# Norm sums taken one token to a partition and turned back, and GpSimd's three scalings issued in a row

## The chip, the core and the metric

The kernel runs on one core of one Trainium2 chip. The metric is device time in microseconds (us), from the start of an execution to its end; smaller is better. One execution was also recorded by the hardware profiler, and all rows below come from it. The engines are named as the profile names them: PE is TensorE (matmuls), PEld its weight loads, DVE VectorE, ACT ScalarE, POOL GpSimd, SP the engine that issues the transfers.

## The reference, cut to what matters

A two-layer backbone over 256 latent tokens (`x`) and 256 context tokens (`xc`), width 1024. Each layer is FFN, token mixer, FFN; in front of each of the three stands an RMS norm with a learned shift and scale. Layer 0 mixes with latent attention (MLA), which norms two of its inner projections as well; layer 1 with windowed attention. In the last layer the context stream is dropped after the mixer.

```python
def rms_norm(x, g):
    xf = x.astype(jnp.float32)
    y = xf * lax.rsqrt(jnp.mean(xf * xf, axis=-1, keepdims=True) + EPS)
    return (y * g.astype(jnp.float32)).astype(x.dtype)

def modulate(h, shift, scale):
    return h * (1.0 + scale) + shift
...
    for layer in range(DEPTH):
        x = x + 0.5 * mx[2] * swiglu(modulate(rms_norm(x, norm_g[layer, 0]), mx[0], mx[1]), ...)
        xc = xc + 0.5 * mc[2] * swiglu(modulate(rms_norm(xc, norm_g[layer, 0]), mc[0], mc[1]), ...)
        hx = modulate(rms_norm(x, norm_g[layer, 1]), mx[3], mx[4])
        hc = modulate(rms_norm(xc, norm_g[layer, 1]), mc[3], mc[4])
        ox, oc = mla_mixer(hx, hc, ...) or swa_mixer(hx, hc, ...)
        x = x + mx[5] * ox
        x = x + 0.5 * mx[8] * swiglu(modulate(rms_norm(x, norm_g[layer, 2]), mx[6], mx[7]), ...)
        if not last:
            ...
    return rms_norm(x, final_norm_g)
```

In `mla_mixer` the projections `cq` (512 wide) and `ckv` (256 wide) go through `rms_norm` before they are multiplied on.

## The kernel before

Everything is held transposed: features on the 128 partitions, tokens along the free axis. `xs[d]` (d = 0 to 7) holds 128 features of all 512 tokens; columns 0 to 255 are the latent stream, called stream 0 here, columns 256 to 511 the context stream, stream 1. Every product is done as three matmuls of two-part numbers (`mm3`, lines 210 to 212: high by high, high by low, low by high), so each weight tile is split into `whi` (ACT, line 182) and `wlo` (DVE or POOL, line 183), and each activation likewise.

`closing` runs the last projection of a sublayer tile by tile, adds it to `xs[d]` (line 357), and lets ACT square the new `xs[d]` (line 236) while POOL adds the squares up (line 242). The last two tiles are held back and done stream by stream. As soon as stream 0 is complete, the norm of the next sublayer starts for it while PE still works on stream 1: `rstd_of` multiplies the squares by a matrix of ones (line 221), so that every partition gets the sum for every token, ACT takes the root over 128x256 (line 223), DVE the reciprocal over 128x256 (line 225). `stream` then scales the eight tiles k = 0 to 7. For k = 2, 5, 7 (`POOL`) this is a product on POOL (line 287), gain and shift on ACT (line 288), and the split on ACT (line 182) and POOL (line 183); for the others DVE does product and gain (line 290), ACT adds the shift into the high part (line 185), and DVE makes the low part (line 186). Then `leading` multiplies the first weight tiles of the next sublayer by these inputs, k by k.

The norm appears fourteen times in this form. Six places in the program hold ten of them: place 1 (about 402 to 430 us, in front of MLA), place 2 (619 to 645, in front of the second FFN), place 3 (998 to 1020, first FFN of layer 1), place 4 (1374 to 1400, in front of the windowed attention) with both streams each, place 5 (1533 to 1550, last FFN, stream 0 alone) and place 6 (from 1734, the final norm, stream 0 alone, whose scaled tiles are written out). The other four are the inner norms of MLA (`Normed.finish`, 442 to 470). The very first norm of the program is coded apart.

A scheduler orders the instructions of each engine when the program is built; on the chip each engine runs its own list in order and waits for semaphores of the others. Buffers come from rings: 8 PSUM banks, 7 `strip` tiles of 128x256, 46 `r2k` tiles.

Of the kernel before, what the change touches and what calls it, by code (L numbers as in the profile page):

```python
# [10 lines left out]
F32 = mybir.dt.float32  # L11
# [3 lines left out]
ALU = mybir.AluOpType  # L15
# [22 lines left out]
def hybrid_backbone_kernel(ctx, tc, t, out):  # L38
# [6 lines left out]
    def bank(shape=(P, 512)):  # L45
        return ps.tile(list(shape), F32, tag="bank", name="bank")

    def r2k(n=512, parts=P):
        return ring.tile([parts, n], F32R, tag="r2k", name="r2k", bufs=46)
# [4 lines left out]
    def strip():  # L54
        return ring.tile([P, T], F32, tag="strip", name="strip", bufs=7)
# [107 lines left out]
    def behind(ins):  # L163

        return tc.issue_after(ins.ins) if ins else nullcontext()
# [48 lines left out]
    def pair(p, *idx):  # L214
        return p[0][idx], p[1][idx]

    def rstd_of(parts, dim, after=None):

        b = bank()[:, :T]
        for i, p in enumerate(parts):  # L220
            nc.tensor.matmul(b, lhsT=ones, rhs=p, start=(i == 0), stop=(i == len(parts) - 1))
        r = strip()
        nc.scalar.activation(r, b, AF.Sqrt, scale=1.0 / dim, bias=eps)  # L223
        with behind(after):
            nc.vector.reciprocal(r, r)  # L225
        return r

    class Squares:

# [19 lines left out]
    class Sublayer:  # L249
# [12 lines left out]
                self.squares[s].add(xs[d][:, SL[s]])  # L262

        def rstd(self, s):
            return rstd_of(self.squares[s].parts, D, self.end)

        def place(self, s, k):
            if k == len(self.hs):
# [8 lines left out]
            return mod[self.l][:, s, c:c + 1]  # L277

        def stream(self, s):
            r = self.r.get(s) or self.rstd(s)  # L280
            ys = {}

            def scale(k):
                ys[k] = r2k(T).bitcast(F32)
                x = xs[k][:, SL[s]]
                if k in POOL:
                    nc.gpsimd.tensor_tensor(ys[k], x, r, ALU.mult)  # L287
                    nc.scalar.activation(ys[k], ys[k], AF.Identity, bias=self.shift(s, k), scale=self.gain(s, k))
                else:
                    nc.vector.scalar_tensor_tensor(ys[k], x, self.gain(s, k), r, ALU.mult, ALU.mult)  # L290

            scale(0)
            for k in range(KT):
                if k + 1 < KT:
                    scale(k + 1)
                hi, lo = self.place(s, k)
                if k in POOL:
                    split(hi, lo, ys[k], engine=nc.gpsimd)
                else:
                    self.end = split(hi, lo, ys[k], bias=self.shift(s, k))  # L300
            return r[:, 0:1]
# [38 lines left out]
    class Final(Sublayer):  # L340


        def stream(self, s):
            r = self.rstd(s)
            for k in range(KT):
                y = strip()
                if k in POOL:
                    nc.gpsimd.tensor_tensor(y, xs[k][:, SL[s]], r, ALU.mult)
                    nc.scalar.activation(y, y, AF.Copy, scale=fng[:, k:k + 1])
                else:  # L350
                    nc.vector.scalar_tensor_tensor(y, xs[k][:, SL[s]], fng[:, k:k + 1], r, ALU.mult, ALU.mult)
                nc.sync.dma_start(out[k], y)
# [186 lines left out]
    def mla(sl, nxt):  # L539
# [3 lines left out]
        class Normed:  # L543
# [12 lines left out]
                    self.squares[s].add(raw[:, SL[s]])  # L556

            def finish(self, s):
                r = rstd_of(self.squares[s].parts, self.n * P)
                for i, x in enumerate(self.tiles):  # L560
                    if s == 0:
                        self.pairs.append((r2k(), r2k()))
                    hi, lo = self.pairs[i]
                    y = strip()
                    nc.vector.scalar_tensor_tensor(y, x[:, SL[s]], self.g[:, i:i + 1], r, ALU.mult, ALU.mult)
                    split(hi[:, SL[s]], lo[:, SL[s]], y)
                return r[:, 0:1]

# [414 lines left out]
```

## Time and profile before

| | |
|---|---|
| median of 3 runs | 1747.94 us (1747.8 to 1748.0) |
| profiled execution, its own time | 1748.32 us |
| its span, first to last instruction | 1746.3 us |
| PE busy | 1688.0 us (97%) |
| DVE, ACT, POOL busy | 62%, 38%, 11% |

The span is 2.0 us shorter than the execution's time; that rest lies before the first and after the last instruction. A busy share is an average over the whole program. Apart from the first 65 us and the inside of the windowed attention (1405 to 1510 us), PE idles for more than a moment only at the places named above, so what the norms cost is read there, from PE's idle time and from what ended it.

### The profile page before, as it was taken

How to read it: one execution, taken by the hardware profiler on the slowest of the kernel's cores; microseconds unless marked ns; L12 is line 12 of the kernel's file. 1: busy time of each engine (PE TensorE's matmuls, PEld its weight loads, DVE VectorE, ACT ScalarE, POOL GpSimd, SP SyncE). 2: the span in 40 equal slices, each digit the busy share in tenths (PEclk: the TensorE clock that was granted, in tenths of full speed). 3: DMA queues.
4: the chain of work that ended last, by engine and by line, in shares of the span. 5: the costliest groups of instructions: out<-in, count | busy, mean ns of one | idle time of the engine just before them, and what ended most of it. 6: DMA issues, size and time to landing. Idle time of an engine off the chain costs nothing.

```text
span 1746.3 us, 23850 instructions
## 1 busy us (share of the span) xinstructions
PE 1688.0 (97%) x9428; PEld 1439.0 (82%) x9428; DVE 1088.4 (62%) x1592; ACT 669.7 (38%) x1121; POOL 187.6 (11%) x183
## 2 busy tenths in 40 slices
PE   7999999999999999999999999999999989989997
PEld 4688888888788898888888888888888888889997
DVE  4877576646767467856946474645433679755554
ACT  4422222234556353222222342222222577554443
POOL 1000000004132130000000220000000452110001
PEclk9999999999999999999999999999999999999999
DMA  9556355431212126644735245634322221145552
GB/s 339 173 199 192 129 192 180 157 121 55 85 49 73 49 84 201 206 145 156 219 126 170 93 143 183 216 114 158 103 97 86 89 84 51 55 145 181 173 191 96
DMA packets 72831, 242.71 MB, mean 139 GB/s; under 512 B 8848, under 2 KB 10640, under 8 KB 72720
## 3 DMA queue, kind: packets, MB, share of 16 engines
q1 hardware_dynamic: 72720, 241.20, 41.9%
q8 instruction: 74, 1.21, 0.3%
q14 instruction: 37, 0.30, 0.1%
HBM read 240.11 MB, written 1.05 MB: 138 GB/s over the span
## 4 chain that ended last, share of the span: by engine, by line
PE 55%; DVE 4%; ACT 2%; issue 1%; POOL 1%; DMA 0%; POOLq 0%; ACTq 0%; DVEq 0%
PE bank L210 18%; PE bank L211 18%; PE bank L212 18%; DVE small L444 1%; DVE r2k L183 1%; PE bank L157 1%; DVE wlo L183 0%; DVE strip L225 0%; POOL r2k L183 0%; ACT r2k L182 0%; POOL r2k L287 0%; DVE small L457 0%; PE bank L102 0%; ACT whi L182 0%; DVE x L464 0%
## 5 line engine op out<-in xcount | busy, mean ns | idle before, releaser
L210 PE MATMUL bank<-r2k,whi 128*128 128x512 f32 (+1 forms) x2610 | 918.4, 353 | 9.3 <-ACT r2k L185 4.7
L211 PE MATMUL bank<-r2k,whi 128*128 128x512 f32 (+1 forms) x2610 | 915.3, 351 | 9.8 <-POOL r2k L183 6.1
L212 PE MATMUL bank<-r2k,wlo 128*128 128x512 f32 (+1 forms) x2610 | 912.2, 350 | 4.1 <-POOL wlo L183 2.2
L182 ACT CAST whi<-wraw 128x1024 fp32r<-128x1024 f32 (+1 forms) x313 | 321.7, 1028 | 886.8 <-PE bank L211 527.8
L210 PEld LDWEIGHTS bank<-r2k,whi 128*128 128x128 f32 x2610 | 494.6, 190 | 89.9 <-ACT whi L182 9.2
L211 PEld LDWEIGHTS bank<-r2k,whi 128*128 128x128 f32 x2610 | 496.2, 190 | 78.8 <-POOL r2k L183 8.6
L212 PEld LDWEIGHTS bank<-r2k,wlo 128*128 128x128 f32 x2610 | 495.7, 190 | 69.4 <-POOL wlo L183 3.0
L183 DVE TENSOR_TENSOR wlo<-wraw,whi 128x1024 fp32r<-128x1024 f32 (+1 forms) x302 | 362.9, 1204 | 134.7 <-ACT whi L182 124.7
L151 DVE SCALAR_TENSOR_TENSOR big<-modraw,conds,big 128x1024 f32<-128x1024 f32 x196 | 242.2, 1279 | 13.9 <-DMA modraw<-in_modw 13.3
L357 DVE SCALAR_TENSOR_TENSOR x<-bank,mod,x 128x256 f32<-128x256 f32 x192 | 85.7, 478 | 179.9 <-PE bank L212 179.9
L242 POOL TENSOR_TENSOR strip<-strip 128x256 f32<-128x256 f32 x64 | 65.2, 1032 | 1137.1 <-ACT strip L236 1110.4
L418 DVE TENSOR_TENSOR tmp<-bank,tmp 128x512 f32<-128x512 f32 (+1 forms) x88 | 54.9, 624 | 179.6 <-PE bank L212 177.7
L183 DVE TENSOR_TENSOR r2k<-bank,r2k 128x512 fp32r<-128x512 f32 (+2 forms) x107 | 62.0, 616 | 18.2 <-ACT r2k L182 17.9
L182 ACT CAST r2k<-bank 128x512 fp32r<-128x512 f32 (+2 forms) x107 | 52.4, 541 | 16.4 <-PE bank L212 15.7
L183 DVE TENSOR_TENSOR r2k<-tmp,r2k 128x512 fp32r<-128x512 f32 (+1 forms) x88 | 54.4, 618 | 1.5 <-ACT r2k L182 1.4
L182 ACT CAST r2k<-tmp 128x512 fp32r<-128x512 f32 (+1 forms) x88 | 49.7, 566 | 9.9 <-DVE tmp L418 9.5
L416 ACT ACTIVATE tmp<-bank 128x512 f32<-128x512 f32 (+1 forms) x88 | 47.3, 538 | 6.8 <-PE bank L212 6.8
L444 DVE TENSOR_REDUCE small<-bank 128x1 f32<-128x512 f32 (+1 forms) x64 | 37.7, 614 | 0.3 <-PE bank L645 0.2
L236 ACT ACTIVATE strip<-x 128x256 f32<-128x256 f32 x80 | 30.5, 410 | 17.9 <-DVE x L357 17.0
L225 DVE RECIPROCAL strip<-strip 128x256 f32<-128x256 f32 x14 | 24.5, 1750 | 19.9 <-ACT strip L223 19.9
L186 DVE SCALAR_TENSOR_TENSOR r2k<-r2k,mod 128x256 fp32r<-128x256 f32 x45 | 30.3, 696 | 8.7 <-ACT r2k L185 8.5
L450 ACT ACTIVATE tmp<-bank,small 128x512 f32<-128x512 f32 x32 | 21.9, 688 | 18.4 <-DVE small L446 12.3
(152 smaller groups left out, 1067.1 us busy)
## 6 DMA issues: line engine op xcount, KB each, us to landing
wraw<-in_win SPq DMA_DIRECT2D x172, 512.0 KB, 3.5
modraw<-in_modw SPq DMA_DIRECT2D x128, 512.0 KB, 4.2
wraw<-in_wout SPq DMA_DIRECT2D x64, 448.0 KB, 3.3
wraw<-in_wout SPq DMA_DIRECT2D x32, 512.0 KB, 3.5
r2k<-in_modo SPq DMA_DIRECT2D x32, 256.0 KB, 5.7
wraw<-in_mwo SPq DMA_DIRECT2D x8, 512.0 KB, 3.5
wraw<-in_swq SPq DMA_DIRECT2D x8, 512.0 KB, 3.5
wraw<-in_swo SPq DMA_DIRECT2D x8, 512.0 KB, 3.4
```

The costliest lines, as they stand in the source:

```text
L151: nc.vector.scalar_tensor_tensor(acc[s], raw, conds[:, kt, s:s + 1], acc[s], ALU.mult, ALU.add)
L182: nc.scalar.copy(hi, src)
L183: return engine.tensor_tensor(lo, src, hi.bitcast(F32), ALU.subtract)
L210: nc.tensor.matmul(o, lhsT=ah, rhs=bh, start=(i == 0), stop=False)
L211: nc.tensor.matmul(o, lhsT=ah, rhs=bl, start=False, stop=False)
L212: nc.tensor.matmul(o, lhsT=al, rhs=bh, start=False, stop=(i == n - 1))
L236: nc.scalar.activation(q, x, AF.Square)
L242: nc.gpsimd.tensor_tensor(self.parts[0], self.parts[0], q, ALU.add)
L357: nc.vector.scalar_tensor_tensor(xs[d][:, SL[s]], o[:, SL[s]], mod[l][:, s, c:c + 1], xs[d][:, SL[s]], ALU.mult, ALU.add)
L416: nc.scalar.activation(sg[:, :w], og[:, :w], AF.Silu)
L418: nc.vector.tensor_tensor(pr[:, :w], ou[:, :w], sg[:, :w], ALU.mult)
L444: nc.vector.tensor_reduce(top[:, j:j + 1], o[:, :w], axis=AX.X, op=ALU.max)
```

## The change

`rstd_of` now uses the squares as the weights of the matmul and one column of ones as the moving operand. The sum for 128 tokens then stands in one column with one token to a partition; two halves of 128 tokens and two parts of squares make four matmuls. Root and reciprocal are taken over 128x2. Each of the two columns is then spread over 128 columns and turned by a PE transpose against the identity, which gives the old layout in the upper half of the same bank (`wide`). ACT copies it to a `strip` (`kept`). The first tile (k = 0) is scaled from the bank, the others from the strip. In `stream`, POOL's three products for k = 2, 5, 7 are written in a row, right behind tile 0. The fixed position of the reciprocal behind an earlier instruction (`behind(after)`) is gone.

```diff
-    def rstd_of(parts, dim, after=None):
-
-        b = bank()[:, :T]
-        for i, p in enumerate(parts):
-            nc.tensor.matmul(b, lhsT=ones, rhs=p, start=(i == 0), stop=(i == len(parts) - 1))
-        r = strip()
-        nc.scalar.activation(r, b, AF.Sqrt, scale=1.0 / dim, bias=eps)
-        with behind(after):
-            nc.vector.reciprocal(r, r)
-        return r
+    def rstd_of(parts, dim):
+
+
+        b = bank()
+        for j in range(2):
+            for i, p in enumerate(parts):
+                nc.tensor.matmul(b[:, j:j + 1], lhsT=p[:, j * P:(j + 1) * P], rhs=ones[:, 0:1], start=(i == 0), stop=(i == len(parts) - 1))
+        r = small(2)
+        nc.scalar.activation(r, b[:, 0:2], AF.Sqrt, scale=1.0 / dim, bias=eps)
+        nc.vector.reciprocal(r, r)
+        wide = b[:, T:]
+        for j in range(2):
+            nc.tensor.transpose(wide[:, j * P:(j + 1) * P], r[:, j:j + 1].to_broadcast([P, P]), ident)
+        kept = strip()
+        nc.scalar.copy(kept, wide)
+        return wide, kept
...
         def stream(self, s):
-            r = self.r.get(s) or self.rstd(s)
+            wide, r = self.r.get(s) or self.rstd(s)
             ys = {}
 
             def scale(k):
-                ys[k] = r2k(T).bitcast(F32)
-                x = xs[k][:, SL[s]]
                 if k in POOL:
-                    nc.gpsimd.tensor_tensor(ys[k], x, r, ALU.mult)
                     nc.scalar.activation(ys[k], ys[k], AF.Identity, bias=self.shift(s, k), scale=self.gain(s, k))
                 else:
-                    nc.vector.scalar_tensor_tensor(ys[k], x, self.gain(s, k), r, ALU.mult, ALU.mult)
+                    ys[k] = r2k(T).bitcast(F32)
+                    nc.vector.scalar_tensor_tensor(ys[k], xs[k][:, SL[s]], self.gain(s, k), r if k else wide, ALU.mult, ALU.mult)
 
             scale(0)
+            for k in POOL:
+                ys[k] = r2k(T).bitcast(F32)
+                nc.gpsimd.tensor_tensor(ys[k], xs[k][:, SL[s]], r, ALU.mult)
             for k in range(KT):
...
             def finish(self, s):
-                r = rstd_of(self.squares[s].parts, self.n * P)
+                wide, r = rstd_of(self.squares[s].parts, self.n * P)
...
-                    nc.vector.scalar_tensor_tensor(y, x[:, SL[s]], self.g[:, i:i + 1], r, ALU.mult, ALU.mult)
+                    nc.vector.scalar_tensor_tensor(y, x[:, SL[s]], self.g[:, i:i + 1], r if i else wide, ALU.mult, ALU.mult)
```

The lists of the engines differ only around the norms; that of SP, which issues the transfers, is the same row by row. Three stretches show what moves. Rows of the new kernel carry its own line numbers: 221 became 223 (sums) and 229 (transposes), 223 became 225 (root), 225 became 226 (reciprocal), 231 is the new copy, 236 became 242, 242 became 248, 287 became 299 (POOL's product), 288 became 291, 290 became 294.

POOL at place 2, stream 0, before; the first row adds a square of stream 1 (`strip`), L287 multiplies by the norm, L183 makes a low part (`r2k`):

```order
L242 TENSOR_TENSOR strip<-strip 128x256 [waits Activation_49]
L287 TENSOR_TENSOR r2k<-x,strip 128x256 [waits DVE_49,PE_49]
L183 TENSOR_TENSOR r2k<-r2k 128x256 [waits PE_49,Activation_49]
L287 TENSOR_TENSOR r2k<-x,strip 128x256 [waits PE_49]
L183 TENSOR_TENSOR r2k<-r2k 128x256 [waits PE_49,Activation_49]
L287 TENSOR_TENSOR r2k<-x,strip 128x256
L183 TENSOR_TENSOR r2k<-r2k 128x256 [waits PE_49,Activation_49]
```

POOL at the same place in the new kernel:

```order
L248 TENSOR_TENSOR strip<-strip 128x256 [waits Activation_49,Pool_49] x9
L299 TENSOR_TENSOR r2k<-x,strip 128x256 [waits DVE_49,Activation_49]
L299 TENSOR_TENSOR r2k<-x,strip 128x256 [waits DVE_49] x2
L183 TENSOR_TENSOR r2k<-r2k 128x256 [waits PE_49,Activation_49]
L248 TENSOR_TENSOR strip<-strip 128x256 [waits Activation_49,Pool_49]
L183 TENSOR_TENSOR r2k<-r2k 128x256 [waits PE_49,Activation_49] x2
```

The three products moved ahead of stream 1's square and of the low parts that stood between them.

ACT at place 2, stream 0, from the first shift (L185) on, before:

```order
L185 ACTIVATE r2k<-r2k,mod_90 128x256 [waits DVE_49] x2
L288 ACTIVATE r2k<-r2k,mod_90,coefA_92 128x256 [waits Pool_49]
L182 CAST r2k<-r2k 128x256 [waits Activation_49]
L182 CAST whi<-wraw 128x1024 [waits DMAHW6_49,PE_49]
L185 ACTIVATE r2k<-r2k,mod_90 128x256 [waits DVE_49]
L236 ACTIVATE strip<-x 128x256 [waits DVE_49]
L185 ACTIVATE r2k<-r2k,mod_90 128x256 [waits DVE_49]
L288 ACTIVATE r2k<-r2k,mod_90,coefA_92 128x256 [waits Pool_49]
L182 CAST r2k<-r2k 128x256 [waits Activation_49]
```

ACT at the same place in the new kernel, from the copy (L231) on:

```order
L231 COPY strip<-bank 128x256 [waits PE_49,Pool_49]
L291 ACTIVATE r2k<-r2k,mod_90,coefA_92 128x256 [waits Pool_49]
L185 ACTIVATE r2k<-r2k,mod_90 128x256 [waits DVE_49]
L291 ACTIVATE r2k<-r2k,mod_90,coefA_92 128x256 [waits Pool_49]
L185 ACTIVATE r2k<-r2k,mod_90 128x256 [waits DVE_49]
L291 ACTIVATE r2k<-r2k,mod_90,coefA_92 128x256 [waits Pool_49]
L182 CAST r2k<-r2k 128x256 [waits Activation_49]
L242 ACTIVATE strip<-x 128x256 [waits DVE_49]
```

The gain-and-shift steps for POOL's tiles, which wait for POOL, moved ahead of the shifts of tiles 0 and 1, and the cast of tile 2 behind all three of them.

DVE at place 5, from the reciprocal on, before:

```order
L225 RECIPROCAL strip<-strip 128x256 [waits Activation_49]
L290 SCALAR_TENSOR_TENSOR r2k<-x,coefA_93,strip 128x256 [waits DVE_49]
L290 SCALAR_TENSOR_TENSOR r2k<-x,coefA_93,strip 128x256
L186 SCALAR_TENSOR_TENSOR r2k<-r2k,mod_91 128x256 [waits Activation_49] x2
L290 SCALAR_TENSOR_TENSOR r2k<-x,coefA_93,strip 128x256 x2
```

DVE at the same place in the new kernel:

```order
L226 RECIPROCAL small<-small 128x2 [waits Activation_49]
L294 SCALAR_TENSOR_TENSOR r2k<-x,coefA_93,bank 128x256 [waits Activation_49]
L294 SCALAR_TENSOR_TENSOR r2k<-x,coefA_93,strip 128x256
L186 SCALAR_TENSOR_TENSOR r2k<-r2k,mod_91 128x256 [waits Activation_49] x2
L294 SCALAR_TENSOR_TENSOR r2k<-x,coefA_93,strip 128x256 x2
```

The scaling of tile 0, which reads the bank, waits for ACT, one ACT instruction later than the reciprocal in front of it does: that is the copy into the strip.

## Rows read from the trace of the kernel before

**Rows 1.** The page's part 1: busy time, share of the span, instructions.

```profile
PE 1688.0 (97%) x9428; PEld 1439.0 (82%) x9428; DVE 1088.4 (62%) x1592; ACT 669.7 (38%) x1121; POOL 187.6 (11%) x183
```

**Rows 2.** PE's waits, the longest of a norm: who for whom, us, times, longest.

```profile
PE bank L211 <- POOL r2k L183: 6.1, 10, 1.2
```

**Rows 3.** Stretches: us, busy time by engine, PEclk (granted clock), DMA share, GB/s.

```profile
400.00:425.00 25.00, 22.84 (x165) 20.94 (x164) 14.58 (x21) 12.20 (x24) 9.17 (x11) 1.00 0.22 74
425.00:440.00 15.00, 12.98 (x94) 11.25 (x93) 12.17 (x17) 9.58 (x20) 5.36 (x6) 1.00 0.10 36
440.00:478.00 38.00, 38.00 (x187) 30.81 (x186) 28.79 (x47) 20.28 (x40) 4.63 (x5) 1.00 0.26 84
623.00:633.00 10.00, 8.90 (x68) 8.09 (x66) 7.88 (x15) 7.66 (x15) 4.83 (x6) 1.00 0.00 0
627.00:635.70 8.70, 6.33 (x43) 5.29 (x42) 5.42 (x8) 4.72 (x10) 4.86 (x5) 1.00 0.17 55
635.80:639.20 3.40, 3.40 (x16) 3.22 (x15) 1.75 (x1) 0.47 (x1) 0.00 (x0) 0.50 0.45 159
1380.00:1392.00 12.00, 9.71 (x67) 8.17 (x66) 11.21 (x15) 6.96 (x14) 6.90 (x9) 1.00 0.27 89
1530.00:1550.00 20.00, 14.66 (x94) 13.04 (x94) 11.45 (x16) 11.54 (x20) 7.02 (x8) 0.83 0.24 80
```

**Rows 4.** Groups by line and shape: count, busy us, mean ns, idle before.

```profile
L225 DVE RECIPROCAL strip<-strip 128x256 f32<-128x256 f32 x14 | 24.5, 1750 | 19.9 <-ACT strip L223 19.9
...
L221 PEld LDWEIGHTS bank<-strip,ones 128*128 128x128 f32 x56 | 9.5, 193 | 3.6 <-ACT strip L236 2.1 <-POOL strip L242 0.2
...
L223 ACT ACTIVATE strip<-bank,eps 128x256 f32<-128x256 f32 x14 | 6.6, 472 | 15.0 <-PE bank L221 15.0
...
L459 DVE RECIPROCAL small<-small 128x2 f32<-128x2 f32 x32 | 5.2, 162 | 8.9 <-ACT tmp L450 8.5
...
L456 ACT ACTIVATE small<-small,c_sink 128x2 f32<-128x2 f32 x16 | 4.7, 294 | 0.0
...
L102 PEld LDWEIGHTS bank<-c_ident,tmp 64*128 64x128 f32 x16 | 1.3, 138 | 1.4 <-issue 1.4
...
L791 ACT COPY tmp<-bank 128x256 f32<-128x256 f32 x2 | 0.7, 374 | 0.0
```

**Rows 5.** Timeline, PE: a norm's two sums; two transposes. Start, us.

```profile
422.09 0.28 PE L212 MATMUL bank<-r2k,wlo 128*128 128x256 f32 x1
422.21 1.02 PE L221 MATMUL bank<-strip,ones 128*128 128x256 f32 x4
...
683.27 0.39 PE L212 MATMUL bank<-r2k,wlo 128*128 128x512 f32 x1
683.50 0.60 PE L102 MATMUL bank<-c_ident,tmp 128*128 128x128 f32 x4
```

**Rows 6.** Timeline, weight loads of two small float32 transposes (64 columns moving).

```profile
1062.40 0.33 PEld L102 LDWEIGHTS bank<-c_ident,tmp 64*128 64x128 f32 x4 [0.35 <-issue]
```

**Rows 7.** Timeline, POOL at place 2, stream 0.

```profile
625.23 0.92 POOL L287 TENSOR_TENSOR r2k<-x,strip 128x256 f32<-128x256 f32 x1
...
631.00 0.92 POOL L287 TENSOR_TENSOR r2k<-x,strip 128x256 f32<-128x256 f32 x1
633.07 1.65 POOL L183 TENSOR_TENSOR r2k<-r2k 128x256 fp32r<-128x256 f32 x1 [1.15 <-DVE wlo L183]
```

**Rows 8.** Timeline at places 2 and 5: root, reciprocal, and the first work behind.

```profile
621.12 0.47 ACT L223 ACTIVATE strip<-bank,eps 128x256 f32<-128x256 f32 x1 [0.85 <-PE bank L221]
...
1536.20 0.46 ACT L223 ACTIVATE strip<-bank,eps 128x256 f32<-128x256 f32 x1
1536.69 1.75 DVE L225 RECIPROCAL strip<-strip 128x256 f32<-128x256 f32 x1 [0.97 <-ACT strip L223]
1539.56 0.80 PE L210 MATMUL bank<-r2k,whi 128*128 128x256 f32 x2 [4.03 <-ACT r2k L185]
...
1547.85 0.39 PE L211 MATMUL bank<-r2k,whi 128*128 128x256 f32 x1 [0.42 <-POOL r2k L183]
```

More of the change, by code (lines that the diff above doesn't have):

```diff
@@ L264, in rstd @@
         def rstd(self, s):
-            return rstd_of(self.squares[s].parts, D, self.end)
+            return rstd_of(self.squares[s].parts, D)
         def place(self, s, k):
@@ L343, in stream @@
         def stream(self, s):
-            r = self.rstd(s)
+            _, r = self.rstd(s)
             for k in range(KT):
```

## The prediction

> **What bounds the kernel now.** I read the page's busy times first. PE works 1688.0 us of the 1746.3 us span [rows 1], so 58 us are all that a shorter chain can win unless PE's own work shrinks. The waits of PE come next: the largest that belongs to norms is for POOL's low parts (line 183), 6.1 us in ten pieces [rows 2]; the longest single one is 4.03 us for the first shifted tile at place 5 [rows 8]. Then the stretches, to see where that idle time lies [rows 3]. PE idles 25.00 − 22.84 = 2.16 us at place 1 under stream 0's norm and 2.02 us under stream 1's; 2.37 us at place 2, which place 3 repeats nearly to the row; 2.29 us at place 4; 5.34 us at place 5. Around MLA's four inner norms (440 to 478) it idles 0.00 us. At place 6 nothing is left for PE; the chain itself ends the program. So ten norms can give something back and four can only cost.
>
> The same stretches show the granted clock. From 635.8 to 639.2 us it was 0.50, that is 1.2 instead of 2.4 GHz, with PE busy all the time, behind a stretch with 2.37 us of idle [rows 3]. Work that takes 3.4 us at half clock takes 1.7 at full, so this drop costs 1.7 us. Place 3 has one more like it, at the same point. At place 5 the mean clock is 0.83 over 20 us, which is 20 × 0.17 × 2 = 6.8 us at half clock, partly idle.
>
> **The reciprocal's chain.** Old: root 0.47, reciprocal 1.75, hand-over 0.04 [rows 4, 8], together 2.3 us from the sums to a usable norm. New: root over 128x2, for which the nearest row is another two-column ACT step, 0.29; reciprocal over 128x2, 0.16, the same shape in the softmax; two transposes, 0.60 from first start to last end [rows 4, 5]; the copy of a 128x256 bank, 0.37 [rows 4]; four hand-overs, some 0.05 each. Sum 1.6 us, 0.7 less. Tile 0's direct read of the bank gives nothing on top: in the new order DVE waits for the copy before that read, as the rows of DVE in the section on the change show. Had it not, tile 0 would come 0.4 us earlier.
>
> **PE's own work.** A norm's two old sums cost PE 0.86 us: four records that end at 422.21 + 1.02 = 423.23, where the matmul ahead ended at 422.37 [rows 5]. Two transposes cost 683.50 + 0.60 − 683.66 = 0.44 us by the same reading [rows 5]. The four new sums stream one column each, so their eight records (float32 takes two) are bound by loading 128 weight columns. The trace has no such matmul. From below: in the four small transposes at 1062.40 the weight loads start (0.33 − 0.14)/3 = 0.063 us apart [rows 6], 0.14 being one load [rows 4]. From above: a weight load of the old sums takes 0.193 us if nothing overlaps [rows 4]. I take 0.063, the same float32 load of 128 columns with little streaming behind it: 8 × 0.063 + 0.44 − 0.86 = +0.08 us a norm, with 0.193 +1.12 us. Fourteen norms: +1.2 us, at most +15.7.
>
> The Trainium skill (TensorE: Matmul & The Clock Gate, section "LDWEIGHTS (loading the stationary operand)") puts a load at columns / 1.2, so about 107 ns for 128 columns; the loads of [rows 6] start closer together than that. By that rule a norm would cost PE 0.86 + 0.44 − 0.86 = 0.44 us more, 6.2 us over fourteen.
>
> Where the transposes stand matters too, because PE runs its list in order and would stop at them for DVE. At places 1 to 4 stream 0's stand five products (0.6 us) behind the sums, and root plus reciprocal with hand-overs need about 0.6: at most 0.1 or 0.2 us of waiting each, which I count in the gains below. In MLA ten or seven long products (2.3 or 1.6 us) lie between, and DVE has at most one weight's low part ahead of the reciprocal. I count no wait there.
>
> **POOL and ACT at place 2, the pattern of places 1 to 4 (stream 0).** The root can start at 621.1 as before [rows 8]: the scheduler puts nine products instead of six between the two groups of sums, which the cheaper sums pay for. The norm is usable at 621.1 + 1.6 = 622.7. POOL's three products now follow at once, 0.92 each [rows 7]: 623.6, 624.5, 625.5, where the first started at 625.23 and the last at 631.00 before [rows 7]. But ACT's list now has a step for POOL's first tile ahead of the shift of tile 0, so nothing but the copy runs before 623.6; from there its fifteen instructions of this stretch take 7.7 us [rows 3] and the last cast ends at 631.3. POOL's last low part ends at 632.2 to 633.0 (0.92 like its other operations, or 1.65 beside DVE's weight splits as now [rows 7]); before it ended at 633.07 + 1.65 = 634.72, and PE waited for it. The input is 1.7 to 2.5 us earlier, PE has 2.37 us of idle to give; with some 0.5 us of waits left in between I count 1.8 us. Places 3 and 4 have like idle and the same lists around POOL: 1.8 each; place 1 has a little less: 1.6. Sum 7.0.
>
> Stream 1 at place 1 (2.02 us) gains little: there DVE now does four scalings in a row, beside POOL's three, before the first low part, so what the norm wins is spent in DVE's list. I count 0.2. At places 2, 3, 4 stream 1 is covered by the products of the third and fourth weight tiles or the next ones, and gains nothing.
>
> **Place 5.** The root starts at 1536.20, held by the load of ACT's table, not by the sums [rows 8]. The norm is usable at 1537.8 instead of 1538.44. Yet tile 0's shift now stands behind POOL's first product (0.92) and the ACT step on it (ACT's mean step is 7.66/15 = 0.5 [rows 3]), so PE starts near 1540.0, 0.4 later than 1539.56 [rows 8]. From there all inputs come faster than PE uses them. Its 48 products on them take 0.12 each at full clock, as the starts at 422.09 and 422.21 show [rows 5], 5.8 us in all. If the clock stays at half until about 1543.7 as it does now, 1.85 us of that is done by then and the rest ends at 1547.6. Today the last of these inputs comes at 1547.85 [rows 8] and four products follow, 1548.3. Gain 0.7 to 0.9, I take 0.9 since the last waits of ACT's casts go too. **Place 6** moves as a whole with the norm: 0.7.
>
> **Sum.** Gains 7.0 + 0.2 + 0.9 + 0.7 = 8.8. Costs: the seven norms without idle behind them (four in MLA, stream 1 at places 2 to 4) 7 × 0.08 = 0.6. Net 8.2 us. The execution profiled took 1748.32 (its span of 1746.3 and 2.0 around it), so 1740.1; the median shown, 1747.94, lies 0.4 below, so 1739.7 against it. The two drops to half clock (1.7 each) stand behind idle that shrinks from 2.4 to about 0.5; but place 1 had 2.0 us of idle in 15 and kept its clock [rows 3], so this is not certain either way. I count one of the two gone: **1738.0 us**. DVE loses 14 × 1.6 = 22 us of work, ACT 14 × 0.18 = 2.5 us of roots against 5.2 of copies; neither is the bound. No transfer is added or moved.
>
> **Rivals.**
> *A load of 128 full weight columns sets a pace of its own.* The two large transposes advance by 0.44/4 = 0.11 us a record [rows 5]. If that is their loads' pace and not that of their columns, the extra over 0.063 is 8 × 0.047 × 14 = 5.3 us: 1739.7 + 5.3 = 1745.0, no change that can be told. For it speaks that the trace has no one-column matmul, against it the spacing of [rows 6], where half the columns move. Chance 0.10. The rule of the Trainium skill named above comes to nearly this case.
> *ACT's list eats the gain.* If POOL's products run slow beside DVE (its low part beside DVE took 1.65 us [rows 7]), shifts of tiles 0 and 1 come a microsecond late and PE waits at the start instead of at the end: places 1 to 5 give nothing, place 6 0.7, costs 0.6: 1747.9. Against it: tile 0 and 1 have slack, since PE still works off stream 1. Chance 0.10.
> *Slower.* PE pays in full for the loads, 0.193 each, on its path at every norm: +15.7 − 8.8 = +6.9, 1754.8. It decides from the point where 14 × (8c − 0.42) exceeds 8.8 + 3.5 us, that is c = 0.16 us a load. Loads overlap in every row I read, so 0.06.
> *Forecast as above:* 0.74, with its own range 1733 (both drops and nearly all idle gone) to 1743 (neither drop gone, gains at half at two of the places).
>
> A measurement here can tell about 0.2%, 3.5 us, from no change, so from 1744.4 on it counts as the same. Faster: the forecast's 0.74 and a good third of the first rival's case, which straddles that line: 0.78. Same 0.16, slower 0.06. The range reaches up to the first rival and a little over: 1732 to 1746.
>
> **What would show it.** POOL's products at each place in one row of three, the third over by 626 at place 2; PE's idle there down from 2.37 to under 1 us; PE's time for the four sums near 0.5 us, the weight loads 0.06 apart; DVE's reciprocal at 0.16; PE's first product at place 5 no earlier than 1539.5 counted on the old time axis. Wrong it would be if the sums showed 0.1 us or more a load, if PE waited for DVE at the transposes for more than 0.2 us at a place, or if a new wait of PE for ACT's shifts of tiles 0 and 1 grew to what the wait for POOL was. A clock at half speed in a stretch that is at full speed now would also do it, at half of the stretch's length.

## The result, and the profile after

The changed kernel takes 1735.51 us (median; 1734.44 to 1736.61), the kernel before 1747.97 (1747.8 to 1748.78). The ratio is 0.9933 with a 95% interval of 0.992 to 0.9945: 12.5 us or 0.7% faster, where 1738.0 was predicted. The profiled execution took 1734.44, its span 1732.5.

The page's part 1, the answer to [rows 1]:

```profile
PE 1682.6 (97%) x9512; PEld 1440.9 (83%) x9512; DVE 1065.3 (61%) x1592; ACT 666.9 (38%) x1135; POOL 185.2 (11%) x183
```

The span fell by 13.8 us, PE's busy time by 5.4; the other 8.4 us are idle time that went. PE's waits (who for whom, us, times, longest), against [rows 2]:

```profile
PE bank L210 <- ACT r2k L185: 2.4, 1, 2.4
...
PE bank L229 <- DVE small L226: 2.1, 2, 1.0
...
PE bank L223 <- ACT strip L242: 1.9, 2, 1.0
...
PE bank L211 <- DVE r2k L186: 1.2, 1, 1.2
...
PE bank L211 <- POOL r2k L183: 0.7, 2, 0.4
```

The wait for POOL's low parts fell from 6.1 us in ten to 0.7 in two. New are waits for the reciprocal at the transposes (L229), 1.0 us each at places 5 and 6, where no product stands between.

The stretches that answer to [rows 3], moved to the new time axis by the offset of each place's first sum (columns as there): place 1, MLA, place 2 under stream 0, and what follows it, then place 5.

```profile
398.70:423.70 25.00, 24.41 (x187) 22.84 (x185) 14.40 (x26) 13.91 (x31) 11.29 (x15) 1.00 0.22 74
...
435.70:473.70 38.00, 38.00 (x207) 31.51 (x205) 22.38 (x47) 19.92 (x43) 4.58 (x5) 1.00 0.26 84
623.40:632.10 8.70, 8.27 (x67) 7.81 (x67) 5.62 (x10) 4.15 (x9) 3.28 (x5) 1.00 0.22 64
632.20:635.60 3.40, 3.40 (x31) 3.40 (x30) 3.40 (x5) 3.20 (x8) 2.76 (x4) 1.00 0.37 141
...
1518.00:1538.00 20.00, 15.61 (x110) 14.99 (x109) 10.36 (x16) 11.86 (x22) 6.91 (x8) 0.83 0.25 81
```

PE's idle time at place 2 went from 2.37 to 0.43 us, and the 3.4 us behind it run at a granted clock of 1.00 where [rows 3] has 0.50; PE runs 31 matmuls there instead of 16. Place 3 has lost its half-clock stretch too.

Groups by line and shape (count, busy us, mean ns, idle before), against [rows 4]:

```profile
L223 PEld LDWEIGHTS bank<-ones,strip 128*128 128x128 f32 x112 | 14.3, 191 | 2.6 <-ACT strip L242 2.1 <-POOL strip L248 0.2
...
L229 PE MATMUL bank<-c_ident,small 128*128 128x128 f32 x28 | 6.0, 297 | 2.1 <-DVE small L226 2.1
L231 ACT COPY strip<-bank 128x256 f32<-128x256 f32 x14 | 5.1, 372 | 12.9 <-PE bank L229 12.9
L294 DVE SCALAR_TENSOR_TENSOR r2k<-x,coefA,bank 128x256 f32<-128x256 f32 x9 | 4.3, 478 | 6.8 <-ACT strip L231 6.8
L225 ACT ACTIVATE small<-bank,eps 128x2 f32<-128x2 f32 x14 | 3.6, 258 | 12.3 <-PE bank L223 12.3
...
L226 DVE RECIPROCAL small<-small 128x2 f32<-128x2 f32 x14 | 2.2, 162 | 12.6 <-ACT small L225 12.6
```

Root 0.26 (priced at 0.29), reciprocal 0.16, copy 0.37: these pieces of the chain came as priced or a little below. A norm has eight sum records (112 in 14), but only two transpose records (28 in 14), one to a transpose. DVE waits 6.8 us for ACT's copy before it reads the bank for tile 0, as said.

PE's timeline around one norm, stream 1 of place 2 (start, us):

```profile
629.09 0.28 PE L212 MATMUL bank<-r2k,wlo 128*128 128x256 f32 x1
629.21 0.95 PE L223 MATMUL bank<-ones,strip 128*128 128x1 f32 x8
630.02 0.36 PE L210 MATMUL bank<-r2k,whi 128*128 128x256 f32 x1
630.22 0.28 PE L211 MATMUL bank<-r2k,whi 128*128 128x256 f32 x1
...
630.58 0.28 PE L211 MATMUL bank<-r2k,whi 128*128 128x256 f32 x1
630.71 0.43 PE L229 MATMUL bank<-c_ident,small 128*128 128x128 f32 x2
630.90 0.36 PE L212 MATMUL bank<-r2k,wlo 128*128 128x256 f32 x1
```

The product behind the sums ends at 630.38, the one ahead of them at 629.37. Less the 0.12 us that a product takes, the sums cost 0.89 us, 0.11 a record. By the same reading the transposes cost 630.90 + 0.36 − 630.58 − 0.28 − 0.12 = 0.28 us here, and in MLA, where a product of 512 columns takes 0.23, 463.48 + 0.48 − 463.11 − 0.40 − 0.23 = 0.22:

```profile
463.11 0.40 PE L210 MATMUL bank<-whi,r2k 128*128 128x512 f32 x1
463.34 0.38 PE L229 MATMUL bank<-c_ident,small 128*128 128x128 f32 x2
463.48 0.48 PE L211 MATMUL bank<-wlo,r2k 128*128 128x512 f32 x1
```

A new norm costs PE 1.11 to 1.17 us against 0.86: 0.25 to 0.31 more, not 0.08.

POOL at place 2, and place 5 (timeline rows), against [rows 7, 8]:

```profile
619.13 2.33 POOL L299 TENSOR_TENSOR r2k<-x,strip 128x256 f32<-128x256 f32 x3 [4.41 <-ACT strip L231]
```

```profile
1524.16 0.24 ACT L225 ACTIVATE small<-bank,eps 128x2 f32<-128x2 f32 x1
...
1525.59 0.48 DVE L294 SCALAR_TENSOR_TENSOR r2k<-x,coefA,bank 128x256 f32<-128x256 f32 x1 [0.98 <-ACT strip L231]
...
1526.39 0.60 ACT L291 ACTIVATE r2k<-r2k,mod,coefA 128x256 f32<-128x256 f32 x1 [0.84 <-POOL r2k L299]
1526.90 0.49 ACT L185 ACTIVATE r2k<-r2k,mod 128x256 fp32r<-128x256 f32 x1
...
1527.44 1.22 PE L210 MATMUL bank<-r2k,whi 128*128 128x256 f32 x4 [2.35 <-ACT r2k L185]
```

The three products run in a row and are over at 621.46, which is 625.0 on the old axis (place 2 begins 3.56 us earlier). At place 5 ACT's step for POOL's tile (L291) stands ahead of tile 0's shift; PE starts at 1527.44, on the old axis 1539.48 (offset 12.04).

**Where the time came from.** I cut the program at the first sum of each place and of MLA, by the starts in the timelines, and compared the stretches (us). "Half" adds up the half-clock time from place 1 to place 5, without the one at place 5, which every kernel has (6.8 us, in c1 10.2). The letters are the experiments below.

```
             head   pl.1  MLA    pl.2   pl.3   pl.4   pl.5   pl.6  half
before       406.6  36.3  176.2  379.1  375.8  159.5  200.2  12.6  13.6
changed      405.3  33.3  177.0  375.3  371.8  158.9  199.1  12.0   6.8
changed (d0) 406.9  33.3  177.0  375.3  371.8  158.9  199.1  12.0   6.8
a1           407.3  34.5  177.0  377.2  375.0  161.1  199.1  11.7   6.8
a2           406.7  33.7  176.2  375.8  373.4  161.0  199.8  12.6  10.2
a3           407.0  36.3  176.2  379.1  375.8  161.8  200.2  12.6  17.0
a4           405.5  33.3  176.3  375.3  371.8  157.7  198.6  11.7   3.4
b3           407.1  33.3  177.0  375.3  371.8  158.2  199.4  11.9   6.8
b4           407.0  35.8  176.3  375.8  372.4  160.5  198.8  12.3  13.6
b6           406.9  33.6  181.7  376.3  372.1  159.8  199.2  12.4  13.6
c1           405.8  35.1  181.7  377.2  373.7  160.8  200.6  12.4  10.2
d1           405.0  33.2  176.2  375.2  371.7  157.7  198.5  11.7   3.4
d2           406.8  32.5  175.2  374.4  371.0  157.2  198.9  12.0   3.4
e1           405.9  32.5  178.5  374.4  371.0  157.5  198.6  11.7   6.8
```

The head differs from execution to execution of one kernel (405.3 and 406.9 for the changed one) and tells nothing of the change; the other stretches of the changed kernel repeat to 0.1 us. Apart from the norms' own sums and transposes PE does the same products in each stretch of all these kernels, so the stretches can be compared. Before rounding, the change gives 3.0 at place 1, −0.8 in MLA, 3.8 at place 2, 4.1 at place 3, 0.6 at place 4 with the windowed attention behind it, 1.2 at place 5 and 0.6 at place 6: 12.6 us.

### The profile page after: what moved, and what is told of

Same layout as the page of the kernel before. It is cut to its first block, busy times and chain, and to the rows that moved or that the text cites. A ratio compares the mean times of both kernels' runs of the same rounds, so it can differ in the third digit from the quotient of the medians.

```text
span 1732.5 us, 24034 instructions
## 1 busy us (share of the span) xinstructions
PE 1682.6 (97%) x9512; PEld 1440.9 (83%) x9512; DVE 1065.3 (61%) x1592; ACT 666.9 (38%) x1135; POOL 185.2 (11%) x183
## 3 DMA queue, kind: packets, MB, share of 16 engines
HBM read 240.11 MB, written 1.05 MB: 139 GB/s over the span
## 4 chain that ended last, share of the span: by engine, by line
PE 87%; DVE 5%; issue 2%; ACT 2%; POOL 1%; DMA 1%; SPq 0%; POOLq 0%; ACTq 0%; DVEq 0%
PE bank L210 28%; PE bank L211 28%; PE bank L212 28%; DVE r2k L183 1%; DVE small L451 1%; PE bank L157 1%; DVE wlo L183 1%; DMA r2k<-in_modo 1%; PE bank L479 1%; PE bank L223 0%; POOL wlo L183 0%; PE bank L102 0%; DMA big<-in_win 0%; DVE r2k L294 0%; ACT r2k L182 0%
## 5 line engine op out<-in xcount | busy, mean ns | idle before, releaser
L211 PE MATMUL bank<-r2k,whi 128*128 128x512 f32 (+1 forms) x2610 | 912.4, 350 | 3.1 <-DVE r2k L186 1.2
L211 PEld LDWEIGHTS bank<-r2k,whi 128*128 128x128 f32 x2610 | 495.0, 190 | 68.2 <-DVE r2k L186 1.9
L183 DVE TENSOR_TENSOR wlo<-wraw,whi 128x1024 fp32r<-128x1024 f32 (+1 forms) x302 | 363.1, 1204 | 138.9 <-ACT whi L182 131.9
L183 DVE TENSOR_TENSOR r2k<-bank,r2k 128x512 fp32r<-128x512 f32 (+2 forms) x107 | 62.1, 616 | 18.9 <-ACT r2k L182 18.5
L183 DVE TENSOR_TENSOR r2k<-tmp,r2k 128x512 fp32r<-128x512 f32 (+1 forms) x88 | 54.4, 618 | 1.5 <-ACT r2k L182 1.4
L242 ACT ACTIVATE strip<-x 128x256 f32<-128x256 f32 x80 | 30.6, 410 | 17.8 <-DVE x L364 17.0
L186 DVE SCALAR_TENSOR_TENSOR r2k<-r2k,mod 128x256 fp32r<-128x256 f32 x45 | 28.3, 652 | 8.4 <-ACT r2k L185 7.8
L104 DVE TENSOR_TENSOR mod<-bank,c_modb 128x4 f32<-128x4 f32 x56 | 5.2, 153 | 36.9 <-PE bank L102 36.9
```

Source lines behind the costliest of these rows:

```text
L183: return engine.tensor_tensor(lo, src, hi.bitcast(F32), ALU.subtract)
L211: nc.tensor.matmul(o, lhsT=ah, rhs=bl, start=False, stop=False)
L242: nc.scalar.activation(q, x, AF.Square)
```

## The experiments

The theory (A): two causes add up, POOL's row and the shorter chain, and the half-clock stretches vanish with the idle time. Its rivals: the shorter chain does all (B), or the scheduler's new freedom does part (C).

**a1, the new norm alone.** POOL's products go back into `scale`, as before:

```
 def scale(k):
+    ys[k] = r2k(T).bitcast(F32)
     if k in POOL:
+        nc.gpsimd.tensor_tensor(ys[k], xs[k][:, SL[s]], r, ALU.mult)
         nc.scalar.activation(...)
-for k in POOL:
-    ...
```

> New norm, POOL's three products spread out as before. Theory A (two causes add: the row on POOL fills the idle of places 1 to 4, the shorter chain gives 0.65 us a place, the clock drops go with the idle): 0.65 at each of places 1 to 4, 1.0 at place 5, 0.3 at place 6, less 0.75 in MLA and 3 x 0.26 for stream 1: 2.4 us faster, about 1745.5, PE's wait for POOL's low parts still 3 us or more, the half-clock stretches behind places 2 and 3 still there. Theory B (the shorter chain does all, the row on POOL nothing): 1735.5 and both drops gone.

Measured 1744.28 us, ratio 0.999 (0.9981 to 1.0). Theory A's value; B is out. PE's waits, and the stretch behind place 3:

```profile
PE bank L211 <- POOL r2k L183: 5.2, 7, 1.3
```

```profile
1012.30:1015.70 3.40, 3.40 (x19) 3.40 (x18) 2.79 (x6) 2.66 (x7) 2.12 (x3) 0.51 0.50 166
```

The wait for POOL stays, and the drop behind place 3. That behind place 2 is gone though, with 1.9 us of idle in the 26 us around it (617.5 to 643.5; 2.36 before), while 1.75 us stand ahead of the drop behind place 3: the amount of idle alone does not tell which drop stays. The total hides a miss. Place 4 and what follows took 1.6 us more than before (161.1 against 159.5), where 0.65 less was expected, and the drop that went at place 2 made up for it.

**a2, POOL's row alone.** The kernel before, with the loop over `POOL` of the change's diff and the old norm.

> Old norm, POOL's three products in a row. Theory A: the wait for POOL's low parts falls under 2 us, places 1 to 4 give 1.2 to 1.8 us each, places 5 and 6 nothing, MLA loses nothing, and one or both drops go: 1739 to 1742. Theory B: 1748. A third (the steps of ACT for POOL's tiles now stand ahead of the shifts of tiles 0 and 1 and eat it): 1747 to 1749 with PE waiting for ACT's shift of tile 0.

Measured 1740.83, ratio 0.9967 (0.9956 to 0.9979). Both drops behind places 2 and 3 are gone. PE's waits:

```profile
PE bank L210 <- ACT r2k L185: 7.6, 2, 5.1
...
PE bank L221 <- POOL strip L242: 2.2, 2, 1.1
...
PE bank L211 <- POOL r2k L183: 1.0, 3, 0.4
```

The row takes away the wait for POOL's low parts by itself. But the third theory has its part: at places 4 and 5 PE now waits 2.5 and 5.1 us for tile 0's shift, which stands behind ACT's steps for POOL's tiles. With the old norm POOL starts 0.8 and 0.9 us later behind the place's first sum than in the changed kernel, and at place 4 its three products take 3.28 us instead of 2.32; that lands on the first product. At place 4 the wait is followed by one more half-clock stretch (3.4 us from 1390.4). And at places 1 and 3 PE waits 1.1 us each for POOL's sum of squares (L221 for L242), a wait that the changed kernel doesn't have. So the row alone gives the larger part, and with the shorter chain these waits go or shrink: from place 4 to place 5 each half alone loses some 1.6 us (161.1 and 161.0 against 159.5), and the two together gain 0.6. How much the pair adds to its parts stays open: by the ratios a1 and a2 make 1.7 + 5.8 = 7.5 us of the change's 11.7, by the stretches without the head 4.2 + 7.3 = 11.5 of 12.6 (where each of the two counts the drop at place 2), and executions of the kernel before lay up to 5.9 us apart on that chip (1742.51 to 1748.37).

**a3, the reciprocal set free.** The kernel before without `with behind(after)`.

> The kernel before, where the reciprocal is merely no longer held behind the last shift of the stream ahead. Theory A and B: no change, 1747 to 1749. Theory C (part of the gain is that the scheduler may place the reciprocal freely): faster by over 3 us.

Measured 1750.82, ratio 1.0022 (1.0011 to 1.0033): a little slower, where theories A and B had no change. Only the stretch of place 4 changes, by 2.35 us: the half-clock time there grows (6.8 us from 1397.6, 3.4 from 1442.0, against 6.8 from 1437.9 before). Theory C is out for the kernel before: the freed reciprocal alone gains nothing there. The changed kernel with the position held was not run.

**a4, the old norm in MLA.**

```
-wide, r = rstd_of(self.squares[s].parts, self.n * P)
+wide, r = rstd_old(self.squares[s].parts, self.n * P)   # the norm of before, returned as (r, r)
```

> The changed kernel with the old norm in MLA's four inner norms alone. Theory A (a new norm costs PE 0.26 us more, and in MLA nothing hides that): 0.75 to 1.0 us faster than the changed kernel, 1734.6. Rival (the old reciprocal of 1.75 us on DVE costs MLA as much as PE saves): 1735.5 or more.

Measured 1732.54, ratio 0.9922 (0.9907 to 0.9936). MLA's stretch falls from 177.0 to 176.3, the value of before to 0.1. By the ratios the run is 1.9 us faster than the changed kernel, by the stretches 2.6, more than expected. The rest of that is 1.1 us from place 4 to place 5, where 3.4 us less run at half clock, and 0.5 and 0.3 at places 5 and 6, which the edit doesn't touch; why those two gain was not traced.

**b3, ACT's steps for POOL's tiles issued later.** `scale` skips POOL's tiles, and the step moves into the branch that splits them.

> The changed kernel with ACT's gain-and-shift step of a POOL tile issued where that tile is split, so behind the shifts of tiles 0 and 1. Theory D (these steps, put ahead of the shifts, cost 0.4 us at place 5's start): PE's longest wait at place 5 falls from 2.35 us to below 2.0, the stretch from place 5's first sum to place 6's first sum from 199.1 us to 198.5 to 198.8, else nothing; 1735. Rival (ACT's own order doesn't matter, the shift waits for DVE): no difference at place 5.

Measured 1735.31, ratio 0.9926 (0.991 to 0.9943). The edit didn't reach what it was for: the scheduler put ACT's step ahead of tile 0's shift as before, and PE's wait at place 5 is 2.35 us again. The stretch is 199.4, 0.4 more than the changed kernel's: no gain. Whether that order costs 0.4 us at place 5 stays open.

**b6, the same with two banks.** The column is turned into two banks; ACT copies one, DVE reads the other:

```
-wide = b[:, T:]
+wide, spare = b[:, T:], bank()[:, :T]
+for o in (wide, spare):
     for j in range(2):
-        nc.tensor.transpose(wide[...], ...)
+        nc.tensor.transpose(o[...], ...)
-nc.scalar.copy(kept, wide)
+nc.scalar.copy(kept, spare)
```

> As the run before, and the column is turned twice, into two banks, so that tile 0's scaling on DVE reads one bank while ACT copies the other. Cost 0.22 us on PE a norm: 7 covered norms, 1.5 us. Theory E (the copy holds up tile 0 by 0.4 us and that shows where nothing else is late): another 0.3 us off PE's wait at place 5, nothing elsewhere, in all 1 us slower than the run before, 1736. Rival (tile 0 read early is worth it at places 1 to 4 too): as fast as the run before or faster.

Measured 1742.34, ratio 0.9975 (0.9965 to 0.9986): 7 us slower than b3, not 1. With four transposes the scheduler puts them sooner behind the sums, and PE waits there for the reciprocal, which was the prediction's sign of failure. PE's waits from 438 to 484 us, in MLA:

```profile
PE bank L230 <- DVE small L226: 3.2, 4, 1.4
```

MLA's stretch grows by 4.7 us over the changed kernel: 3.2 of waiting, 4 × 0.22 of transposes, and a half-clock stretch from 445.0 (that is less than the pieces add up to; some of it overlaps). Places 2 and 4 lose 1.0 us each besides. Place 5's wait stays at 2.4 us.

**b4, the old norm wherever products cover it.** a4's edit, and in `leading` `self.r[1] = rstd_old(...)`.

> The changed kernel with the old norm in MLA's four norms and for stream 1 at places 1 to 4. By the prices of the changed kernel's trace (0.26 us a norm on PE, eight norms): 2.1 us faster than the changed kernel less what place 1's stream 1 had won (0.5): about 1733.5 to 1734, a ratio of 0.992. Rival (the long reciprocal of 1.75 us comes back onto DVE beside stream 0's scaling and delays it): slower than with MLA alone turned back, 1735 or more, with PE waiting for DVE's or POOL's low parts at places 2 to 4.

Measured 1740.24, ratio 0.996 (0.9945 to 0.9975): the rival, and by more than it asked. PE's waits at place 1 (414 to 428 us), and what follows:

```profile
PE bank L210 <- ACT r2k L185: 1.7, 1, 1.7
PE bank L211 <- DVE r2k L186: 1.0, 1, 1.0
```

```profile
428.20:431.60 3.40, 3.40 (x18) 3.40 (x17) 2.43 (x4) 1.13 (x3) 1.81 (x2) 0.50 0.00 0
```

The prediction let stream 1 gain 0.2 us at place 1 and nothing at places 2 to 4. Against a4, stream 1's old norm costs 2.6 us at place 1, 0.5 and 0.6 at places 2 and 3, where PE waits 0.6 us each for DVE's low part (L186), and 2.8 at place 4 and behind: 6.5 us. Of that 5.1 are clock, for b4 spends 10.2 us more at half of it (3.4 each at place 1, at place 4 and in the windowed attention).

**c1, the sums made twice.** `for j in (0, 1, 0, 1)` in the loop of the sums.

> The changed kernel with each norm's four sums made twice (the second time the same numbers into the same columns): eight records more a norm. At 0.112 us a record 0.9 us a norm: in full in MLA, at stream 1's norms and at places 5 and 6 (10 norms, 9 us), about half at stream 0 of places 1 to 4, where some idle is left (2 us): 1746 to 1747. At 0.063 us a record, as the prediction had it: 1740 to 1742.

Measured 1749.42, ratio 1.0014 (1.0004 to 1.0023): the higher price, and some 3 us on top of it. Against the changed kernel places 1 to 3 pay 1.8 to 2.0 us each, the full price for the norms of both streams, where half was expected for stream 0; and 3.4 us more run at half clock. PE's timeline and two windows in MLA:

```profile
440.82 3.63 PE L223 MATMUL bank<-ones,strip 128*128 128x1 f32 x32
444.32 0.77 PE L210 MATMUL bank<-r2k,whi 128*128 128x512 f32 x1
```

```profile
438.00:444.20 6.20, 6.20 (x44) 5.04 (x43) 1.77 (x3) 1.31 (x2) 0.00 (x0) 1.00 0.53 175
444.30:447.70 3.40, 3.40 (x10) 2.72 (x10) 0.17 (x1) 0.26 (x1) 0.00 (x0) 0.51 0.35 140
```

32 records take 444.32 − 440.82 = 3.50 us, 0.11 each. And behind them the granted clock falls to 0.51, although PE was never idle: what ran ahead of it were sums of one moving column a record.

**d0, the changed kernel again**, beside the next two on one chip.

> The changed kernel once more, beside the next two on one chip: 1734 to 1737, a ratio of 0.993, the half-clock stretches behind places 2 and 3 absent again and one in the windowed attention. Rival (the two drops are a matter of the single execution, not of the idle that is gone): one or both come back, 1.7 us each.

Measured 1735.06, ratio 0.9932 (0.9917 to 0.9947). All stretches but the head repeat, and the drops are missing again. With the old order of places 2 and 3 both drops stand in two profiles, of the kernel before and of a3. So in these four profiles they go with the kernel. That they do so in every execution is not shown: executions of the kernel before had mean granted clocks from 0.989 to 0.993 on a1's chip.

**d1, the loop over parts outside.** a4, and the sums' loops exchanged (`for i, p in enumerate(parts): for j in range(2):`). In this order both halves' sums are open in one bank at a time, and part of the sums is lost; only the time is read.

> MLA's four norms old, and the four sums of the new ones ordered by part and then by half of the tokens, so that both halves of the part that is early are summed before the late part comes: behind the late part 4 records instead of 6. At 0.112 us a record 0.22 us off the chain at places 5 and 6 and less elsewhere: 0.4 us faster than with MLA old alone, ratio 0.992. Rival (at the half clock of place 5 a record takes longer, so more): 0.6 us.

Measured 1732.69, ratio 0.992 (0.9903 to 0.9936), as a4 without it; places 5 and 6 take 198.5 and 11.7 us, as in a4 (198.6 and 11.7). All stretches together are 0.4 us shorter than a4's, none of them by more than 0.1. No gain that can be told. The Trainium skill (PSUM — Partial Sum Buffer, section "The four PSUM rules") has the matmul that opens a group clear the marks of its whole bank, so what the other half had summed is overwritten at its next part; the lost sums agree with that, and no run here takes it further.

**d2, the sums in fp32r.** Squares are written as fp32r, and two columns of ones stand in for one. A norm then has four records of sums instead of eight, if an fp32r sum takes one:

```
+one = const.tile([P, 2], F32R, name="one")
+nc.scalar.copy(one, ones[:, 0:2])
-nc.tensor.matmul(b[:, j:j + 1], lhsT=p[:, j * P:(j + 1) * P], rhs=ones[:, 0:1], ...)
+nc.tensor.matmul(b[:, 2 * j:2 * j + 2], lhsT=p[:, j * P:(j + 1) * P].bitcast(F32R), rhs=one, ...)
-nc.scalar.activation(r, b[:, 0:2], AF.Sqrt, ...)
+nc.scalar.activation(r, b[:, 0:4:2], AF.Sqrt, ...)
```

> [...] At 0.112 us a record 0.45 us less a norm on PE: 7 covered norms, stream 1 at place 1 and the chains at places 5 and 6, 10 x 0.45 = 4.5 us, about 1731, ratio 0.9905. Rival 1 (an fp32r weight load costs as much as the two float32 ones): 1735.5. Rival 2 (the shorter sums leave PE waiting at the turns in MLA, where root and reciprocal then end later than PE comes to them): about 1734.

Measured 1730.3 (1729.99 to 1730.64), ratio 0.9905 (0.989 to 0.992): the forecast's ratio, 0.7 us below its time, and the fastest of all. One group in MLA:

```profile
460.62 0.50 PE L225 MATMUL bank<-one,strip 128*128 128x2 f32 x4
460.98 0.49 PE L212 MATMUL bank<-whi,r2k 128*128 128x512 f32 x1
```

Four records for eight, 0.50 us from first start to last end for 0.95. MLA's stretch falls by 1.8 us (four norms at 0.45), places 1 to 3 by 0.8 each (two norms). The total came out by other terms than expected, though: places 5 and 6, counted at 0.45 each, gave 0.1 together, and 1.7 us came from place 4 to place 5, where 3.4 us less run at half clock.

**e1, both.** d2, with MLA's four norms old but in fp32r.

> Sums in fp32r as in the run before, and MLA's four norms in the old form, their two sums in fp32r too (two records of 256 columns, 0.12 us each, 0.24 us a norm). Against 0.45 + 0.22 = 0.67 us a new norm in fp32r: 4 x 0.43 = 1.7 us off the MLA stretch, 1728.5, ratio 0.9895. Rival (the reciprocal of 1.75 us, back on DVE's list in MLA, is late once the sums no longer cover it): no gain or a loss of some tenths, 1730 to 1731.

Measured 1732.28, ratio 0.9913 (0.9899 to 0.9926): the rival, and more. PE's waits in MLA (436 to 476 us):

```profile
PE bank L508 <- ACT r2k L184: 1.9, 1, 1.9
```

With only 0.24 us of sums, PE comes to the rotary permutation (L508) before its input is there, and waits 1.9 us; a half-clock stretch follows at 447.2. MLA takes 178.5 us instead of 175.2. DVE's list has two reciprocals of 1.75 us (from 440.61 and 443.26) ahead of the scalings, and casts of the scaled tiles stand in ACT's list ahead of the cast that L508 waits for. So the old norm is cheaper on PE and dearer in DVE's list, and which of the two counts changes as soon as PE gets faster.

## Why the prediction was right, point by point

**The chain.** Predicted 1.6 us from the sums to a usable norm. At place 2 the last sum ends at 617.60 and POOL starts at 619.13 (its row is above): 1.5. Right, and so is the wait of tile 0 for the copy.

```profile
616.82 0.78 PE L223 MATMUL bank<-ones,strip 128*128 128x1 f32 x6
```

**POOL's row at places 1 to 4.** The mechanism was right: third product over at 625.0 on the old axis (626 was the sign), idle at place 2 down from 2.37 to 0.43. a1 and a2 show that the row is the larger part and that it works in full only with the shorter chain. The sizes: net of stream 1's cost I had 1.7 at places 2 and 3; without the clock they gave 2.1 and 2.4. Place 1 gave 3.0 instead of 1.8: stream 1, which I let win 0.2 because DVE's four scalings in a row would eat it, went from 2.02 us of idle to one wait of 1.2 (L211 for DVE in the waits above). b4 says the same from the other side.

**PE's own work.** This term failed, in both halves. I took 0.063 us a weight load from the small transposes of [rows 6]; the sums took 0.11 us a record, in the changed kernel and doubled in c1. The rule of the Trainium skill (TensorE: Matmul & The Clock Gate, section "LDWEIGHTS (loading the stationary operand)"), columns / 1.2, makes an estimate of 107 ns for 128 columns, and the sums agree with it. The row was the wrong one: it shows transposes, and its loads fill 64 rows of the array (64*128 there, 128*128 in the sums). Whether that is why they came closer together wasn't tried. And I read 0.44 us for two transposes from a group of four records at [rows 5]. A float32 transpose is one record (L229 above), so those were four, as are the four at [rows 6], and a pair costs 0.22 to 0.28. Together +0.25 to +0.31 a norm instead of +0.08, with two errors partly against each other. Rival 1 had the price of a load right and its result, 1745.0, wrong, since it kept the 0.44 and counted no half-clock stretch as gone. In MLA the four norms set PE back by 1.05 us: the first product of 256 columns behind them started 29.01 us after MLA's first sum (442.86) before, and 30.06 after it (438.55) now.

```profile
471.87 0.28 PE L210 MATMUL bank<-r2k,whi 128*128 128x256 f32 x1
```

```profile
468.61 0.28 PE L210 MATMUL bank<-r2k,whi 128*128 128x256 f32 x1
```

At the end of the stretch 0.75 of it are left, where 0.32 were forecast; a4 gives that back. The forecast also charged only seven norms, those that it saw without idle behind them. c1 (8 records more a norm) and d2 (4 fewer) moved places 1 to 3 by the price of both streams' norms, so stream 0's pay there too.

**The clock.** I counted one of two half-clock stretches as gone; both went, at places 2 and 3, 1.7 us more than forecast. The forecast said that this was not certain either way, and nothing in its working tells why both should go: this part of the gain is luck.

**Place 4 and what follows.** I counted 1.8 for the place, and nothing behind. From place 4's first sum to the windowed attention's first long wait (1424.57 before, 1411.33 after) the lead grew from 11.46 to 13.24 us: 1.78, as forecast. By place 5's first sum it is 12.04, so the windowed attention takes 1.2 us back. Its new waits for the inputs of the rotary permutation (2.5 us in four pieces against 0.5 in one; a1 has them too, a2 does not) are not where the lead goes, for behind the last new one, at 1427.35, the gain since place 4's first sum is still 1.76. It goes in two steps. The half-clock stretch ends only 11.63 us earlier (1433.11 against 1444.74), so work that ran at full clock before falls into it: 0.7 us. And PE's wait for one split of DVE grows from 0.91 to 1.37 us (before, then after):

```profile
1464.99 0.36 PE L210 MATMUL bank<-r2k,big 128*128 128x256 f32 x1 [0.91 <-DVE r2k L183]
```

```profile
1452.97 0.36 PE L210 MATMUL bank<-r2k,big 128*128 128x256 f32 x1 [1.37 <-DVE r2k L183]
```

a4 has the same waits there, but 3.4 us at half clock instead of 6.8, and keeps a gain of 1.7 (157.7 against 159.5). That half of the step, that a gain at place 4 reaches the end, was wrong; what sets the length of the half-clock stretch is open.

**Places 5 and 6.** PE's first product came at 1539.48 on the old axis, where 1540.0 was said and 1539.5 as the earliest; the gains are 1.2 instead of 0.9, and 0.6 instead of 0.7.

**Sum.** Against the forecast's terms: place 1 +1.2, MLA −0.4, places 2 and 3 +1.0, the second clock drop +1.7, place 4 with the windowed attention −1.1, places 5 and 6 +0.2. That is 2.6 us more than the 9.9 forecast; 12.6 were measured.

Two of the forecast's own signs of being wrong came: the sums showed 0.11 us a load, where 0.1 was the sign, and PE waited 1.0 us for DVE at the transposes of places 5 and 6 each, where 0.2 was. The first is the failed price above, and larger gains elsewhere covered it. The second was not foreseen, but at these two places PE has no product to do before the norm is there, and both still gained. So the time came out for the reasons given, the row on POOL and the shorter chain, but its nearness to 1738.0 owes something to errors of opposite sign.

## What to carry to other kernels

A price on the bounding engine wants a row of the same kind: the same records to an operation, the same rows and columns loaded. The nearest other row was off by a factor of 1.8 here, and a doubled copy of the disputed work settled it in one run (c1). An edit that brings inputs earlier is worth the idle time of its place plus whatever the clock does behind it, and one half of such an edit alone (a2), or a part of it taken back (b4, e1), can move the wait to another engine. Of the versions run, the change with its sums in fp32r is the fastest, 1730.3 us.

## What the hardware showed unasked

The granted clock fell without any idle time of PE: behind 3.5 us of one-column sums it was 0.51 (c1). A float32 sum took two records of 0.11 us each, an fp32r sum with two moving columns one of 0.11 (d2), and a float32 transpose one, of 0.11 to 0.14 us. Two drops of the clock with 2.4 us of idle ahead of them vanished at 1.9 us in one place (a1, place 2) and at 2.0 in the other (a2, place 3), but one stayed at 1.75 (a1, place 3); what decides that is open.
